# A two-layer hybrid decoder trunk on one core: layer A's column pairs in seven block products over 12 of 16 k tiles, in two chunks, and the output projections' operands split tile by tile behind the tile ahead

## The chip, the cores and the metric

The kernel runs on one core of a Trainium2 chip. The metric is the device time of one execution in microseconds, the median of several runs. The engines are TensorE (PE; its weight loads are listed as PEld), VectorE (DVE), ScalarE (ACT), GpSimd (POOL) and SyncE (SP), which issues most DMAs.

## The reference

Residual stream of 16 meta tokens and 512 tokens, 2048 channels, 16 heads of 128, float32. Layer A projects to q, f, i and z (four times 2048 columns), runs a gated linear recurrence in chunks of 64, normalizes each head, multiplies by a gate and projects back. Then a shared projection to K, V and forget logits, and layer B, attention with a forget bias, gated and projected back.

```python
def hgrn2_mix(h, g_norm, w_in, g_out, w_out, lb):
    u = rms_norm(h, g_norm) @ w_in
    q, f, i, z = ...                       # 2048 columns each
    fg = lb + (1.0 - lb) * jax.nn.sigmoid(f)
    logf, k, v = jnp.log(fg), 1.0 - fg, i
    ...                                    # chunks of 64, state carried from chunk to chunk
    o = rms_norm(o, g_out.reshape(HG_HEADS, HG_VDIM)).reshape(bsz, L, D_MODEL)
    return (o * jax.nn.silu(z)) @ w_out
```

## The kernel before, in words

**Products.** A float32 product is made of three fp32r matmuls: each operand is split into a high part (ScalarE, a copy that rounds: `w_hi`, `sh`) and a low part (VectorE, the difference: `w_lo`, `sl`), and high x high, high x low and low x high are summed in PSUM (`mm_step`, `mms`). The weights are stationary, 128 x 128; the moving operand is the transposed stream, 16 k tiles of 128 x 528 (`movx`), taken in two halves of 264 columns (`r` 0 and 1).

**Column pairs.** `run_pair` computes two 128-column outputs at once. Over the first 2 x KS = 8 k tiles it pairs even and odd k tiles, the two halves and the two columns, and takes seven block products in place of eight (sums of weight blocks `w_sum` t1 to t4 on one side, sums of the stream `S_a` on the other); over the other 8 it multiplies plainly (`rest`). Layer A takes its columns head by head: (f, i) and (q, z) of heads 2 to 14 are pairs, so are (q, z) of head 1 and (f, q) of head 15; the other columns of heads 0, 1 and 15 are plain (`run_ntiles`).

**Weights.** `Weights` streams blocks of up to 128 x 512 float32 through eight raw buffers (`w_raw`, SyncE's queue, in a fixed order), makes the sums (`get_t1`, `get_t2`, `get_t4`: VectorE, but t2's second step on GpSimd, `s.ge`), splits each unit (`split_one`, `flush`), and hands it to TensorE (`get`). A raw buffer is loaded again when the last unit that reads it is split. Units are split ahead by `split_ahead` = 2 and the extra slots of `more` (3 in layer A).

**Order.** All engines but SyncE keep the order in which the code is written out, and that is set by a planner: after each few matmuls `tick` lets `W.step` emit weight work and then each generator in `bg` (the steps of the recurrence: `head_f`, `head_q`, `head_z`, `mix`, `head_pe1`, `head_pe2`) emit as much as `fits`. A generator that needs a tile in use waits with `take`; a product that needs one calls `spin`.

**Sums of the stream.** `sums_a` (`pair_sums`) builds them once, while heads 0 and 1 run.

**Output projections.** The gated heads `G[k]` are the moving operand of layer A's output projection (`movg`) and the stationary one of layer B's (`movo`). `LazySplit` splits them: `movg.upto(NH - 1)` takes 15 of them in one go after the last product of layer A, and `movo` takes each when `o_step` asks for it, two ahead.

Of the kernel before, what the change touches and what calls it, by code (L numbers as in the profile page):

```python
# [7 lines left out]
F32 = mybir.dt.float32  # L8
# [18 lines left out]
KS = 4  # L27
KB = 4
# [191 lines left out]
class Weights:  # L220
# [59 lines left out]
    def add_pair(self, w, c, kps, rest):  # L280

        b = {}

        def block(e, n):
            b[e, n] = self.add_src(
                w[:2 * kps * P, c[n]:c[n] + P].rearrange("(j e p) n -> e p j n", e=2, p=P)[e], kps, P)

        m = kps * P
        key = len(self.units)
        t3, t2 = (key, 3), (key, 2)  # L290

        def plain(e, n):
            return self.add_unit(lambda s: s.raw[b[e, n]], [b[e, n]], m, P)
# [5 lines left out]
        def get_t2(s):  # L299
            for t in (t3, t2):  # L300
                s.sums[t] = s.alloc(f"w_sum{t[1]}", 512, F32)
            op(s.ve, s.sums[t3], s.raw[b[1, 1]], s.raw[b[0, 1]], ALU.subtract)
            return op(s.ge, s.sums[t2], s.sums[t3], s.raw[b[0, 0]], ALU.add)

        def get_t1(s):
            return op(s.ve, s.raw[b[0, 1]], s.raw[b[0, 1]], s.raw[b[0, 0]], ALU.subtract)

        def get_t4(s):
            t = s.sums.pop(t2)
            return op(s.ve, t, s.raw[b[1, 0]], t, ALU.subtract)  # L310

        block(0, 0)
        us = [plain(0, 0)]
        block(1, 1)
        block(0, 1)
        us.append(self.add_unit(get_t2, [b[1, 1], b[0, 1], b[0, 0]], m, P))
        us.append(self.add_plain(*rest[0][0]))
        us.append(self.add_unit(lambda s: s.sums.pop(t3), [], m, P))
        us.append(self.add_unit(get_t1, [b[0, 1], b[0, 0]], m, P))
        block(1, 0)  # L320
        us.append(plain(1, 0))
        us.append(self.add_plain(*rest[0][1]))
        us.append(self.add_unit(get_t4, [b[1, 0]], m, P))
        us.append(self.add_plain(*rest[1][0]))
        us.append(plain(1, 1))
        us.append(self.add_plain(*rest[1][1]))
        return us
# [103 lines left out]
    def step(self):  # L431
# [58 lines left out]
def trunk(  # L490
# [29 lines left out]
    def plan(key, w, c0):  # L520
        nt_unit[key] = [W.add_plain(*t) for t in column(w, c0)]

    def plan_pair(key, w, c):
        nt_unit[key] = W.add_pair(w, c, KS, [column(w, c0, k0=2 * KS) for c0 in c])

# [5 lines left out]
    for h in range(1, NH):  # L531
# [3 lines left out]
        for j, n in ((1, 2), (0, 3))[h == 1:] if h < NH - 1 else ((1, 0),):  # L535
            plan_pair(("a", h, j), awi, [j * D + h * P, n * D + h * P])
    for j in (2, 3):
        plan(("a", NH - 1, j), awi, j * D + (NH - 1) * P)
# [168 lines left out]
    pjb = [0]  # L707
    par = [0]
# [62 lines left out]
    def run_ntiles(keys, mov, nhalf, after=None):  # L771
# [11 lines left out]
        for u in range(nu):  # L783
            parts = [W.get(nt_unit[key][u]) for key in keys]
            for k4 in range(kts):
                k = u * kts + k4
# [3 lines left out]
                for (hi, lo, width), pt in zip(parts, pts):  # L790
                    mm_step(pt, width, (hi, lo), k4, width, xh, xl, k == 0, k == KT - 1, nhalf)
# [5 lines left out]
    def run_pair(key, mov, S_, scale, pool, tags, widths=(L, L), after=None):  # L797
# [1312 lines left out]
```

## Time and profile before

| what | value |
|---|---|
| median of 3 runs | 2013.81 us (2009.59 to 2014.51) |
| the profiled execution | 2009.89 us, span 2008.2 us |
| TensorE busy | 1980.4 us, 99% of the span, 14604 matmuls |
| VectorE, ScalarE, GpSimd busy | 1573.1 (78%), 1000.5 (50%), 319.6 us (16%) |
| granted TensorE clock, mean | 0.997 of full speed |

Layer A's heads lie from about 40 to 838 us, its output projection and what hangs on it from there to about 1050, the K/V columns up to about 1400, layer B to 1825, and its output projection at the end. A row with an arrow reads: output written from inputs; the shape is partitions x elements. In the timeline the bracket names the idle time of the engine before the row and what ended it. All instructions are put down to one line, that of the helper which issues them, so they are told apart by their tiles.

### The profile page before, as it was taken

The page shows a single profiled execution, that of the slowest core. Times are in us where ns is not written, and L with a number is a line of the kernel's source. Part 1 is how long each engine was busy: PE and PEld are TensorE (multiplying, and loading weights), DVE is VectorE, ACT ScalarE, POOL GpSimd, SP SyncE. Part 2 cuts the span into 40 slices and gives each one's busy share as a digit, 9 for nine tenths or more (in the row PEclk, how much of TensorE's full clock was granted, in tenths as well). Part 3 has the DMA queues.
Part 4 walks back from the last instruction along what each step waited for, and adds up shares of the span by engine and source line. Part 5 has one row for each costly group of instructions (what it writes and reads, how often), then busy time and mean ns, then how long its engine had stood idle before and what let it go on. Part 6 is the DMA issues. An engine that isn't in the chain of part 4 may idle for free.

```text
span 2008.2 us, 39614 instructions
## 1 busy us (share of the span) xinstructions
PE 1980.4 (99%) x14604; PEld 1851.0 (92%) x14604; DVE 1573.1 (78%) x3153; ACT 1000.5 (50%) x1869; POOL 319.6 (16%) x429
## 2 busy tenths in 40 slices
PE   8999999999999999999999999999999999999999
PEld 7999999999999999889999999999788888887888
DVE  6878888888888887788788887868677777776965
ACT  6655454545454545544343333323666666666532
POOL 2121111111111111111210000000211111220011
PEclk9999999999999999999999999999999999999999
DMA  8343333434343433446563445446556555565552
GB/s 268 101 113 109 107 112 103 116 101 119 99 120 99 120 99 104 147 132 179 163 197 98 114 123 140 117 119 184 157 159 172 157 155 164 164 166 141 147 167 91
DMA packets 455492, 273.39 MB, mean 136 GB/s; under 512 B 78065, under 2 KB 420577, under 8 KB 455281
## 3 DMA queue, kind: packets, MB, share of 16 engines
q1 hardware_dynamic: 453728, 266.33, 46.6%
q0 software_dynamic: 1536, 4.52, 0.6%
q8 instruction: 115, 1.88, 0.4%
q14 instruction: 81, 0.66, 0.1%
q10 hardware_dynamic: 32, 0.01, 0.0%
HBM read 222.46 MB, written 48.28 MB: 135 GB/s over the span
## 4 chain that ended last, share of the span: by engine, by line
PE 80%; DVE 6%; DMA 5%; ACT 4%; issue 3%; SPq 2%; POOL 0%; ACTq 0%; DVEq 0%; POOLq 0%
PE pj L196 74%; SPq L196 2%; PE o L196 2%; DMA py<-pd 2%; PE tr L196 2%; PE pat L196 2%; DVE w_lo L196 1%; ACT w_hi L196 1%; DVE lg L196 1%; DVE sm L196 1%; DMA pd<-py 1%; DVE kl L196 1%; DMA w_raw<-in_a_w_in_dram 1%; ACT lg L196 1%; ACT D L196 1%
## 5 line engine op out<-in xcount | busy, mean ns | idle before, releaser
L196 PE MATMUL pj<-sh,w_hi 128*128 128x264 f32 (+1 forms) x2484 | 750.2, 315 | 5.2 <-ACT sh L196 2.2
L196 PE MATMUL pj<-sh,w_lo 128*128 128x264 f32 (+1 forms) x2484 | 732.5, 308 | 2.4 <-DVE w_lo L196 2.4
L196 PE MATMUL pj<-sl,w_hi 128*128 128x264 f32 (+1 forms) x2484 | 733.3, 308 | 1.5 <-DVE sl L196 1.5
L196 DVE TENSOR_TENSOR w_lo<-w_raw,w_hi 128x512 fp32r<-128x512 f32 x585 | 429.7, 743 | 84.2 <-ACT w_hi L196 82.3
L196 PEld LDWEIGHTS pj<-sh,w_hi 128*128 128x128 f32 x2484 | 456.8, 189 | 27.7 <-ACT sh L196 3.2
L196 PEld LDWEIGHTS pj<-sh,w_lo 128*128 128x128 f32 x2484 | 455.8, 189 | 24.8 <-DVE w_lo L196 3.1
L196 PEld LDWEIGHTS pj<-sl,w_hi 128*128 128x128 f32 x2484 | 456.6, 189 | 20.4 <-DVE sl L196 2.5
L196 ACT ACTIVATE w_hi<-w_raw 128x512 fp32r<-128x512 f32 x585 | 354.6, 621 | 146.2 <-PE pj L196 104.3
L196 PE MATMUL pj<-sm,w_hi 128*128 128x264 f32 x896 | 172.2, 289 | 0.0
L196 ACT ACTIVATE w_hi<-w_sum 128x512 fp32r<-128x512 f32 x120 | 74.5, 626 | 179.2 <-POOL w_sum L196 93.4
L196 PE MATMUL pj<-kh,w_lo 128*128 128x264 f32 x556 | 142.7, 285 | 0.8 <-DVE w_lo L196 0.8
L196 PE MATMUL pj<-kh,w_hi 128*128 128x264 f32 x556 | 143.5, 286 | 0.0
L196 PE MATMUL pj<-kl,w_hi 128*128 128x264 f32 x556 | 142.8, 285 | 0.0
L196 PEld LDWEIGHTS pj<-sm,w_hi 128*128 128x128 f32 x896 | 138.5, 188 | 1.4
L196 PE MATMUL pj<-sm,w_lo 128*128 128x264 f32 x448 | 127.6, 285 | 0.0
L196 POOL TENSOR_TENSOR w_sum<-w_sum,w_raw 128x512 f32<-128x512 f32 x34 | 51.8, 1522 | 456.0 <-DVE w_sum L196 252.6
L196 ACT ACT_TABLE_LOAD x88 | 112.9, 1283 | 5.9 <-issue 3.1
L196 DVE TENSOR_TENSOR w_lo<-w_sum,w_hi 128x512 fp32r<-128x512 f32 x120 | 90.3, 757 | 13.5 <-ACT w_hi L196 12.6
L196 PEld LDWEIGHTS pj<-kh,w_lo 128*128 128x128 f32 x556 | 98.4, 188 | 1.3 <-DVE w_lo L196 1.3
L196 PEld LDWEIGHTS pj<-kh,w_hi 128*128 128x128 f32 x556 | 98.4, 189 | 0.0
L196 PEld LDWEIGHTS pj<-kl,w_hi 128*128 128x128 f32 x556 | 98.3, 188 | 0.0
L196 PE MATMUL pj<-kh,sh 128*128 128x264 f32 x324 | 87.6, 286 | 0.0
(403 smaller groups left out, 3568.2 us busy)
## 6 DMA issues: line engine op xcount, KB each, us to landing
w_raw<-in_a_w_in_dram SPq DMA_DIRECT2D x256, 256.0 KB, 3.4
w_raw<-in_kv_w_dram SPq DMA_DIRECT2D x128, 256.0 KB, 4.1
w_raw<-in_b_w_in_dram SPq DMA_DIRECT2D x128, 256.0 KB, 3.3
w_raw<-in_a_w_out_dram SPq DMA_DIRECT2D x64, 256.0 KB, 3.8
w_raw<-in_b_w_out_dram SPq DMA_DIRECT2D x64, 256.0 KB, 3.9
xr<-xT SPq DMA_DIRECT2D x16, 264.0 KB, 3.7
h1T<-h SPq DMA_DIRECT2D x16, 264.0 KB, 2.1
kT<-kn SPq DMA_DIRECT2D x16, 264.0 KB, 2.4
```

Source lines behind the costliest of these rows:

```text
L196: ins = f(*args, **kw)
```

## The change

Layer A's pairs take the seven products over 2 x KA = 12 k tiles and the rest over 4. A block of six k tiles is too wide for one buffer, so it comes in two chunks of 128 x 384, and every sum and split is made per chunk; the second chunk's t2 is on VectorE alone, and block (1, 1) is loaded a second time for the last product. Extra slots go from 3 to 2, and sums may be made four units ahead instead of two (in all stages). Head 1 becomes plain in all four columns. The stream's sums are kept for six tile pairs, the fourth of them in place of the even tiles' second halves, which no pair uses (`fourth_sums`, behind head 1; head 2's first pair waits for it in `late`), and head 15's plain column i starts with k tiles 12 to 15 while these halves are made anew from `xT` (`restored`). `head_z` uses the tile `bl` under the token `mixed` in place of a tile of its own. Both output projections' operands are split by a generator (`early`) during the last product ahead: tile k once TensorE's written order has passed k + 1. Pending blocks of layer B's output are counted one by one.

```diff
+KA = 6
 def add_pair(self, w, c, kps, rest):
+        chunks = range(-(-kps // 4))
+        nk = kps // len(chunks)
+        m = nk * P
         def block(e, n):
+            for x in chunks:
+                rows = w[2 * nk * P * x:2 * nk * P * (x + 1), c[n]:c[n] + P]
+                b[e, n, x] = self.add_src(rows.rearrange("(j e p) n -> e p j n", e=2, p=P)[e], nk, P)
+        def get_t2(s, x):
+            for t in (3, 2):
+                s.sums[key, t, x] = s.alloc(f"w_sum{t}{x}", m, F32)
+            op(s.ve, s.sums[key, 3, x], s.raw[b11[x]], s.raw[b[0, 1, x]], ALU.subtract)
+            return op(s.ge if x == 0 else s.ve, s.sums[key, 2, x], s.sums[key, 3, x], s.raw[b[0, 0, x]], ALU.add)
...
+        us += units(get_t4, (1, 0))
+        us.append(self.add_plain(*rest[1].pop(0)))
+        if again:
+            block(1, 1)
+        us += plain(1, 1)
 def step(self):
-            elif self.nr < min(max(self.nh, self.ns + 1) + 2, end + 2, len(self.units)) and self.sums_fit():
+            elif self.nr < min(max(self.nh, self.ns + 1) + 4, end + 4, len(self.units)) and self.sums_fit():
...
+            plan(("a", h, 0), awi, h * P)
+            plan(("a", h, 3), awi, 3 * D + h * P)
+            continue
+        for j, n in ((1, 2), (0, 3)) if h < NH - 1 else ((1, 0),):
+            plan_pair(("a", h, j), awi, [j * D + h * P, n * D + h * P], KA)
+    plan(("a", NH - 1, 2), awi, 2 * D + (NH - 1) * P, KT // UK - 1)
 def run_pair(...):
+        rest(p2, x1, True, () if more else (1,))
+        if late:
+            late()
+        product(p2[0][:, :HALF], s(1, 1), False, not more)
+    def sums_in_place():
+        for i in range(KA):
+            ...
+            yield from parts_of(sa, st[0], st[1])
+            yield from parts_of(xe[:, r0], st[2], st[3])
+    def fourth_sums():
+        for i in range(KA):
+            yield from take("os")
+            ...
+            yield from do(act, hi, x[:, r0], AF.Copy)
+            yield from do(ve.tensor_tensor, lo, x[:, r0], hi.bitcast(F32), op=ALU.subtract)
+    def restored():
+        for i in range(KA):
+            hi, lo = (t[:, HALF:] for t in movx[2 * i])
+            yield from do(act, hi, rx[i], AF.Identity, scale=g)
+            yield from do(ve.scalar_tensor_tensor, lo, rx[i], g, hi.bitcast(F32), ALU.mult, ALU.subtract)
 def head_z(hd, uz):
-        while sums in bg:
-            yield
-        sz = tl("sz")
+        yield from take("mixed")
+        sz = tl("bl")
...
+        free_u("mixed")
 class LazySplit(list):
+        def early(self, n):
+            for k in range(n):
+                while not self.stop and (at_k[0] <= k + 1 or k not in G):
+                    yield
+                if self.stop:
+                    return
+                ...                         # high part on ScalarE, low part on VectorE
...
-            W.more(lambda n, w, dt: sp.tile([P, w], dt, name=n, tag=n), 3, nt_unit["a", NH - 1, 1][-1] + 1)
+            W.more(lambda n, w, dt: sp.tile([P, w], dt, name=n, tag=n), 2, nt_unit["a", NH - 1, 1][-1] + 1)
...
+            movg = LazySplit(L)
+            movg.begin(NH - 1)
             (pt,) = run_ntiles([("a", h, 3)], movx, 2)
-    movg = LazySplit(L)
+    movg.end()
     movg.upto(NH - 1)
...
+        if slot == len(border) - 1:
+            at_k[0] = 0
+            movo = LazySplit(S)
+            movo.begin(NH // 2)
```

What stands in a row on VectorE in the middle of layer A, at the first products of a pair (f, i), before. `w_sum` is a sum of weight blocks, the second of the two made on GpSimd and not seen here; `e`, `kp`, `dp`, `uq` are steps of the recurrence:

```order
L196 TENSOR_TENSOR w_sum_6485<-w_raw 128x512
L196 SCALAR_TENSOR_TENSOR e_6276<-skf,lbt,e_6276 128x528
L196 SCALAR_TENSOR_TENSOR kp<-skf,lbt,bl 128x528
L196 TENSOR_TENSOR dp<-eb 128x4
L196 TENSOR_TENSOR uq<-pj_6304,uq 128x264
L196 TENSOR_TENSOR uq<-pj_6305,uq 128x264
L196 TENSOR_TENSOR uq<-uq,R 128x528
L196 TENSOR_TENSOR w_lo_6522<-w_sum_6486,w_hi_6521 128x512
L196 TENSOR_TENSOR w_lo_6531<-w_raw,w_hi_6530 128x512
L196 TENSOR_TENSOR w_raw<-w_raw 128x512
L196 STREAM_TRANSPOSE y0k<-kp 128x32
L196 STREAM_TRANSPOSE yk<-kp 128x3x4x32
```

And after, at the same place:

```order
L197 TENSOR_TENSOR w_lo_6969<-w_raw,w_hi_6968 128x384
L197 SCALAR_TENSOR_TENSOR e_6697<-skf,lbt,e_6697 128x528
L197 TENSOR_TENSOR w_sum_7002<-w_raw 128x384
L197 TENSOR_TENSOR w_sum_7014<-w_raw 128x384
L197 TENSOR_TENSOR w_sum_7015<-w_sum_7014,w_raw 128x384
L197 TENSOR_TENSOR uz<-pj_6958,uz 128x264
L197 TENSOR_TENSOR uz<-pj_6959,uz 128x264
L197 TENSOR_TENSOR uz<-uz,R 128x528
L197 TENSOR_TENSOR w_lo_7041<-w_sum_7003,w_hi_7040 128x384
L197 TENSOR_TENSOR w_lo_7050<-w_sum_7015,w_hi_7049 128x384
L197 TENSOR_TENSOR w_raw<-w_raw 128x384 x2
L197 TENSOR_TENSOR w_lo_7071<-w_raw,w_hi_7070 128x512
```

Where one sum of 512 stood, there are three of 384, and every low part of a sum comes twice; the steps of the recurrence (`kp`, `dp`) have moved behind them.

On ScalarE at the end of layer A, before (the last four of 15 splits of `g` that stand together, and what follows; `sz` is the last head's gate, `w_hi` are the output projection's weights):

```order
L196 ACTIVATE sh11_11552<-g11_11133 128x528
L196 ACTIVATE sh12_11556<-g12_11135 128x528
L196 ACTIVATE sh13_11560<-g13_11137 128x528
L196 ACTIVATE sh14_11564<-g14_11273 128x528
L196 ACTIVATE w_hi0_11651<-w_raw_11274 128x512
L196 ACTIVATE w_hi1_11660<-w_raw_11331 128x512
L196 ACT_TABLE_LOAD
L196 ACTIVATE sz_11612<-uz_11505 128x528
L196 ACTIVATE w_hi2_11674<-w_raw_11382 128x512
L196 ACTIVATE w_hi3_11706<-w_raw_11425 128x512
```

After, the same splits (`sh4` to `sh12`), while the last product runs; `w_hi` are that product's units and the first of the projection, `osq` the last head's output:

```order
L197 ACTIVATE sh4_12270<-g4_11927 128x528
L197 ACTIVATE w_hi2_12287<-w_raw_11999 128x512
L197 ACTIVATE sh5_12292<-g5_11929 128x528
L197 ACTIVATE sh6_12302<-g6_11931 128x528
L197 ACTIVATE sh7_12317<-g7_11933 128x528
L197 ACTIVATE sh8_12321<-g8_11935 128x528
L197 ACTIVATE sh9_12333<-g9_11937 128x528
L197 ACTIVATE w_hi3_12345<-w_raw_12073 128x512
L197 ACTIVATE sh10_12351<-g10_11939 128x528
L197 ACTIVATE sh11_12363<-g11_11941 128x528
L197 ACTIVATE osq_12376<-os_12373 128x528
L197 ACTIVATE sh12_12379<-g12_11943 128x528
```

They stand ahead of `osq` and among the last product's weights, where all 15 stood behind `osq`.

On ScalarE at the end of layer B, before; `buz` is the last gate's sigmoid, `lg` the softmax exponentials of the last head, `sh` the splits that the output projection needs first:

```order
L196 ACTIVATE lg,sm<-lg,sm 128x144
L196 ACTIVATE aos<-o 128x512
L196 ACTIVATE lg,sm<-lg,sm 128x272
L196 ACT_TABLE_LOAD
L196 ACTIVATE buz<-pj_24330 128x512
L196 ACTIVATE sh_24545<-g_19910 128x512
L196 ACTIVATE sh_24549<-g_20190 128x512
L196 ACTIVATE sh_24553<-g_20417 128x512
L196 ACTIVATE w_hi_24562<-w_raw 128x512
L196 ACT_TABLE_LOAD
L196 ACTIVATE lg,sm<-lg,sm 128x400
```

After:

```order
L197 ACTIVATE w_hi_25313<-w_raw 128x512
L197 ACTIVATE sh_25321<-g_21975 128x512
L197 ACTIVATE aos<-o 128x512
L197 ACTIVATE sh_25343<-g_22327 128x512
L197 ACTIVATE sh_25350<-g_22675 128x512
L197 ACTIVATE sh_25354<-g_22973 128x512
L197 ACT_TABLE_LOAD
L197 ACTIVATE buz<-pj_25165 128x512
L197 ACT_TABLE_LOAD
L197 ACTIVATE lg,sm<-lg,sm 128x144
L197 ACTIVATE w_hi_25392<-w_raw 128x512
L197 ACTIVATE lg,sm<-lg,sm 128x272
```

The splits and the sigmoid stand ahead of the exponentials, which stood in front of both.

## Rows read from the trace of the kernel before

**Rows 1.** Windows: stretch, length; busy us (count) PE, PEld, DVE, ACT, POOL; clock, DMA.

```profile
251.64:756.22 504.58, 504.58 (x4303) 488.54 (x4302) 413.49 (x801) 253.03 (x431) 99.16 (x100) 1.00 0.38 109
1120.00:1160.00 40.00, 40.00 (x332) 40.00 (x331) 34.58 (x76) 14.96 (x31) 2.67 (x4) 1.00 0.41 115
865.00:895.00 30.00, 30.00 (x251) 30.00 (x251) 29.03 (x50) 13.13 (x23) 5.03 (x3) 1.00 0.46 139
```

**Rows 2.** Timeline of DVE: start us, us, instruction; two scans, ten heads apart.

```profile
251.64 1.26 DVE L196 TENSOR_TENSOR_SCAN b<-cmask,sf 128x528 f32<-128x528 f32 x1 [1.45 <-ACT sf L196]
...
756.22 1.26 DVE L196 TENSOR_TENSOR_SCAN b<-cmask,sf 128x528 f32<-128x528 f32 x1 [1.45 <-ACT sf L196]
```

**Rows 3.** Groups of DVE, 200 to 800 us: xcount | busy us, mean ns | idle.

```profile
L196 DVE TENSOR_TENSOR w_lo<-w_raw,w_hi 128x512 fp32r<-128x512 f32 x190 | 136.9, 731 | 23.0 <-ACT w_hi L196 23.0
L196 DVE TENSOR_TENSOR w_lo<-w_sum,w_hi 128x512 fp32r<-128x512 f32 x71 | 54.2, 763 | 11.6 <-ACT w_hi L196 11.0
L196 DVE TENSOR_TENSOR w_sum<-w_raw,w_sum 128x512 f32<-128x512 f32 x24 | 21.3, 889 | 0.0
L196 DVE TENSOR_TENSOR w_sum<-w_raw 128x512 f32<-128x512 f32 x23 | 15.8, 688 | 0.5 <-DMA w_raw<-in_a_w_in_dram 0.5
```

**Rows 4.** Timeline of DVE, two neighbours of 512 columns, and 384 before 528.

```profile
322.11 0.53 DVE L196 STREAM_TRANSPOSE yk<-kp 128x384 f32<-128x384 f32 x1
322.57 0.66 DVE L196 TENSOR_TENSOR uq<-uq,sf 128x528 f32<-128x528 f32 x1
...
340.33 0.68 DVE L196 TENSOR_TENSOR w_sum<-w_raw 128x512 f32<-128x512 f32 x1
340.94 0.68 DVE L196 TENSOR_TENSOR w_lo<-w_raw,w_hi 128x512 fp32r<-128x512 f32 x1
```

**Rows 5.** Waits of DVE, 200 to 800 us: us in total, times, longest.

```profile
DVE w_lo L196 <- ACT w_hi L196: 34.0, 33, 2.9
DVE st L196 <- PE tr L196: 28.0, 12, 4.8
DVE b L196 <- ACT sf L196: 19.6, 11, 2.2
```

**Rows 6.** Groups of POOL and of ACT, 200 to 800 us, as rows 3.

```profile
L196 POOL TENSOR_TENSOR w_sum<-w_sum,w_raw 128x512 f32<-128x512 f32 x23 | 34.3, 1490 | 352.3 <-DVE w_sum L196 205.7 <-ACT bl L196 146.6
...
L196 ACT ACT_TABLE_LOAD x34 | 43.6, 1283 | 0.6
```

**Rows 7.** Timeline of PE where layer A's output projection begins, the waits.

```profile
839.33 0.51 PE L196 MATMUL pj<-sh,w_hi 128*128 128x264 f32 x2 [0.54 <-ACT sh L196]
840.91 0.52 PE L196 MATMUL pj<-sl,w_hi 128*128 128x264 f32 x2 [1.07 <-DVE sl L196]
...
847.33 0.51 PE L196 MATMUL pj<-sh,w_hi 128*128 128x264 f32 x2 [0.58 <-ACT w_hi L196]
850.17 0.51 PE L196 MATMUL pj<-sh,w_lo 128*128 128x264 f32 x2 [2.08 <-DVE w_lo L196]
...
861.32 0.51 PE L196 MATMUL pj<-sh,w_hi 128*128 128x264 f32 x2 [1.63 <-ACT sh L196]
```

**Rows 8.** Windows, behind these waits (columns of rows 1).

```profile
850.00:855.00 5.00, 4.83 (x27) 4.83 (x28) 3.04 (x5) 2.08 (x3) 2.49 (x1) 0.66 0.72 205
```

**Rows 9.** Timelines of ACT and DVE at that place: the splits, the norm.

```profile
838.66 8.11 ACT L196 ACTIVATE sh<-g 128x528 fp32r<-128x528 f32 x15
...
840.17 9.35 DVE L196 TENSOR_TENSOR sl<-g,sh 128x528 fp32r<-128x528 f32 x15
...
851.24 0.72 DVE L196 TENSOR_REDUCE part<-oss 128x17 f32<-128x544 f32 x1
```

**Rows 10.** Layer B's output projection: PE's two waits, the window behind them.

```profile
1828.54 0.51 PE L196 MATMUL pj<-w_hi,sh 128*128 128x512 f32 x1 [2.44 <-ACT sh L196]
...
1829.83 0.50 PE L196 MATMUL pj<-w_hi,sl 128*128 128x512 f32 x1 [0.56 <-DVE sl L196]
...
1830.00:1835.00 5.00, 5.00 (x16) 3.94 (x17) 4.12 (x10) 3.70 (x8) 0.00 (x0) 0.66 0.48 126
```

More of the change, by code (lines that the diff above doesn't have):

```diff
@@ L312, in add_pair, with get_t1, get_t4 @@
+        def get_t1(s, x):
+            return op(s.ve, s.raw[b[0, 1, x]], s.raw[b[0, 1, x]], s.raw[b[0, 0, x]], ALU.subtract)
+        def get_t4(s, x):
+            t = s.sums.pop((key, 2, x))
+            return op(s.ve, t, s.raw[b[1, 0, x]], t, ALU.subtract)
+        again = len(chunks) > 1
+        rest = [list(r) for r in rest]
         block(0, 0)
-        us = [plain(0, 0)]
+        us = plain(0, 0)
         block(1, 1)
+        b11 = [b[1, 1, x] for x in chunks]
         block(0, 1)
-        us.append(self.add_unit(get_t2, [b[1, 1], b[0, 1], b[0, 0]], m, P))
@@ L813, in product @@
         def product(o, xs, first=True, last=True):
-            w = W.get(next(us))
             for i, xx in enumerate(xs):
-                mms(o, w, i, xx, first and i == 0, last and i == KS - 1)
+                if i % nk == 0:
+                    w = W.get(next(us))
+                mms(o, w, i % nk, xx, first and i == 0, last and i == kps - 1)
                 if i % 2:
@@ L834, in done @@
             return u
-        x1, x2 = 2 * KS, 2 * KS + UK
+        x1, x2 = 2 * kps, 2 * kps + UK
+        more = x2 < KT
         pa_, p1 = pj2(), pj2()
@@ L855, in run_pair @@
         add(half(u2, 1), pb[1][:, :HALF], half(u1, 1))
-        product(p1[0][:, :HALF], x(1, 0), False, False)
-        rest(p1, x2, False, (0,))
+        product(p1[0][:, :HALF], x(1, 0), False, not more)
+        if more:
+            rest(p1, x2, False, (0,))
         product(p1[1][:, :HALF], x(1, 1), False)
@@ L989, in __getitem__ @@
             return list.__getitem__(self, k)
+    class Restored(list):
+        def __getitem__(self, k):
+            while k % 2 == 0 and k // 2 < KA and k // 2 >= back_n[0]:
+                spin()
+            return list.__getitem__(self, k)
+    back_n = [0]
     movx = LazyX()
@@ L1354, in trunk @@
             bg.append(tok_major(next(first), 4, "v", hd, "vtok"))
-            while sums in bg:
-                spin()
-            second = run_pair(("a", h, 0), movx, S_a, R, pa, ("uq", "uz"))
+            if h == 1:
+                second = plain(h, (0, "uq"), (3, "uz"))
+            else:
+                second = run_pair(("a", h, 0), movx, S_a, R, pa, ("uq", "uz"), kps=KA)
             bg.append(mix(hd, next(second)))
             bg.append(head_z(hd, next(second)))
+            if h == 1:
+                while sums in bg:
+                    spin()
+                bg.append(fourth)
         else:
@@ L1363, in trunk @@
             gp.append(opened(st_r, "gates_a", side="right"))
+            rx = [gp[0].tile([P, HALF], F32, name=f"rx{i}", tag=f"rx{i}") for i in range(KA)]
+            for i in range(KA):
+                sy.dma_start(rx[i], xT[2 * i][:, HALF:])
+            back = restored()
+            bg.append(back)
             for k, d in gd.items():
@@ L1956, in finish @@
     def finish(n, pts):
-        adding.append(n)
+        adding.extend((n, b) for b in range(4))
         yield from residual(n)
@@ L2008, in wide @@
                 spin()
-            while n == NB3 and NB3 - 1 in adding:
+            while (NB3 - 1, len(pp)) in adding:
                 spin()
```

186 lines of the change are left out of this document (109 added, 77 removed).

## The prediction

> **What bounds the kernel now.** I read the windows first, then the groups of one stage, then the waits. In the ten heads of layer A from 251.64 to 756.22 us TensorE is busy for the whole stretch, and so it is in a stretch of the next stage that holds only 264-column matmuls: 332 in 40 us, 0.1205 us each [rows 1]. The kernel is bound by the number of matmuls. The same row has the second number that counts here: VectorE is busy 413.49 us of those 504.58. The scans that open and close the stretch are ten heads apart [rows 2], so a head takes 50.46 us, of which VectorE works 41.35 and idles 9.11. TensorE stands still in two places only: where the output projection of layer A begins, and where that of layer B begins [rows 7, 8, 10].
>
> **Fewer matmuls.** A pair with seven products over 8 k tiles costs 7 x 4 x 3 = 84 matmuls and 8 x 2 x 2 x 3 = 96 for the rest, 180; over 12 k tiles it costs 7 x 6 x 3 = 126 and 48, 174. 27 pairs (two in each of heads 2 to 14, one in head 15) lose 6 each. Head 1's second pair becomes two plain columns, 192 instead of 180. That is -162 + 12 = -150 matmuls, and the order of the two programs differs by the same 150 rows on TensorE. At 0.1205 us: **-18.1 us**, if TensorE stays fed. A head of two pairs would then take 50.46 - 12 x 0.1205 = 49.0 us.
>
> **What that costs VectorE.** The mean of a group is not what an instruction costs in a queue: a 512-column one took 0.68 us, but the next started 0.61 us after it [rows 4]. So I take 0.08 off each mean of [rows 3]: 0.65 for a low part from a raw block, 0.68 from a sum, 0.81 for the last sum (its mean is lifted by GpSimd, below) and 0.61 for the other two. A 384-column instruction started its successor after 0.46 instead of 0.60, so a piece of three k tiles is 0.13 us cheaper than one of four, not a quarter cheaper [rows 4]. Before, a pair has 8 x 0.65 + 3 x 0.68 + 0.81 + 2 x 0.61 = 9.3 us. After, it has two low parts of 512 and eight of 384 from raw blocks (1.3 + 4.2), six of 384 from sums (3.3), and seven sums of 384, since the second chunk's second sum moves from GpSimd to VectorE (2 x 0.68 + 5 x 0.48 = 3.8): 12.5 us. That is +3.2 us in a pair, 6.4 in a head: VectorE needs 41.35 + 6.4 = 47.7 us of the 49.0. GpSimd gives back a little: its 512-column sum of 1.49 us [rows 6] becomes one of 384, an eighth of its work in a head at most, and the stretch it causes in VectorE's instructions shrinks with it; I count 0.3 us and end at **47.4 of 49.0, 97%**.
>
> So the gain hangs on whether VectorE can live with 1.6 us of idle time in a head where it now has 9.11. Most of that idle time is harmless: in 600 us 34.0 were low parts waiting for ScalarE's high part, which waits until TensorE frees a slot; VectorE is ahead there, and such waits shrink when it is not [rows 5]. The wait of the scan for ScalarE is another kind: VectorE scales uf, ScalarE runs two sigmoids, a table load and a logarithm, and VectorE waits 19.6 us in 11 heads, 1.8 each, with two or three other instructions in between. In the order after, some heads have 4 to 17 instructions there, and some still only two, of 384 columns: these will wait about as long. The nearest row for a loaded VectorE is 865 to 895 us: 29.03 of 30 us busy, also 97%, and TensorE busy throughout [rows 1]. It lasted 30 us, not 600. The look-ahead shrinks as well: the weights may be 5 units beyond the current one before and 4 after (two extra slots instead of three), and most units shrink from 12 matmuls to 9, so 4 x 9 x 0.12 = 4.3 us stand where 5 x 12 x 0.12 = 7.2 stood. Between nothing (the row at 97%) and +2.4 us in a head (were the waits of scan and state, 1.8 and 2.3 us, kept in full: 47.4 + 4.1 - 49.0 = 2.5) I take 0.5, nearer to the row that shows this load: 13 x 0.5 = **+6.5 us**, ends 0 and +32.
>
> One mechanism speaks against a fuller VectorE. The last sum of a pair, which stands beside GpSimd's, takes 0.889 us, its like elsewhere 0.688 [rows 3]. GpSimd works 9.9 us in a head [rows 1], and VectorE is busy 82% of the time; if it never rests, some 1.8 us more of GpSimd's work meet it, and if each costs it half its length (an estimate), its load is 47.4 + 0.9 = 48.3 us. The Trainium skill, "GPSIMD Engine Reference", section "Key points", says the same in general: GpSimd shares its SBUF interfaces with VectorE and contends with instructions that have two SBUF inputs; by that rule the trace's 0.2 us is contention, and the rival below that fills VectorE has it as one of its causes.
>
> **ScalarE, queues, start.** ScalarE gets 14 high parts of 384 and two of 512 instead of 11 of 512, and 20 more table loads; it worked 253 us of 504 [rows 1], and 2.4 us of parts and 20 x 1.28 us of loads in 13 heads [rows 6] make some 4.4 us more in a head: covered. SyncE issues four more weight loads in each pair, and the block (1,1) is read twice, 19% more bytes, at a DMA share of 0.38: covered, as long as the eight raw buffers come free in time (a rival). The sums of x grow from four to six tile pairs and the fourth sums come in head 2: by the start distances above some 12 us more VectorE work in heads 0 to 2, where head 1, now all plain, spares 4.4 and the 9 us of idle time in a head cover the rest; but head 2's first pair waits for the fourth sums before its last product: 0 to +5, I take +1. In head 15 six halves are restored (ScalarE and VectorE, 264 columns, under 0.4 us each) while the product starts at k tile 12, 24 matmuls ahead: 0 to +3, I take +1.
>
> **Layer A's output projection.** Now 15 high parts (8.11 us) and 15 low parts (9.35 us) run in one lump after the last product [rows 9]; the weights' parts stand behind the lump, and TensorE waits 0.54 + 1.07 + 0.58 + 2.08 = 4.3 us [rows 7], then runs at 1.2 GHz for part of 850 to 855: a mean clock of 0.66 means 3.4 us at half speed, 1.7 us lost [rows 8]. The last head's norm waits behind the lump too (its partial sums start at 851.24, [rows 9]), which ends in TensorE's wait of 1.63 at 861.32 [rows 7]. In the order after, twelve of the 15 stand ahead of the last head's output copy, among the last product's weights. All of 4.3 + 1.7 + 1.9 would be -7.9; VectorE has 9.4 us to place within some 12 us of the last product, so I take **-7**, ends 0 and -8.
>
> **Layer B's.** TensorE waits 2.44 + 0.56, then has the half clock for 3.4 us, 1.7 lost [rows 10]: 4.7 us. After, eight tiles are split ahead of the last gate's sigmoid, and that sigmoid ahead of the softmax exponentials; 8 tiles are 20 us of matmuls. **-4.5**, ends 0 and -5. The finer bookkeeping of pending output blocks, and the sums taken up to four units ahead in the other stages, I cost at nothing: TensorE does not wait there.
>
> **The sum**, against the profiled execution of 2009.9: -18.1 + 6.5 + 1 + 1 - 7 - 4.5 = -21.1, so 1988.8. The median of the three runs, 2013.8, lies 3.9 above the profiled one; I add about 1 and forecast **1990 us**.
>
> **Rivals.** *TensorE stays fed*: 97% is enough, as from 865 to 895. Then 6.5 + 2 us do not arise, and the time is 2009.9 - 18.1 - 12 = 1980. *VectorE becomes the bound, mildly*: the waits of scan and state stay, 4.1 us in a head; the head takes 51.5, 13 x 2.5 = 32 us take the place of 6.5: 2014, no change. Against it: those waits shrink when VectorE is late. *VectorE becomes the bound, in earnest*: the overlap with GpSimd brings its load to 48.3 and half of the present idle time, 4.5 us, stays, because an in-order queue also waits for ScalarE, which has the 20 table loads more in front of its high parts. A head takes 52.8, 13 x 3.8 = 49 us replace 6.5: 2031, slower. The point from which it decides: 13 x (head - 49.0) > 18.1 + 11.5 - 2 + 6, a head of over 51.6 us. *The chunks do not stream*: six of eight raw buffers are held by three blocks of two chunks, so loads come late and the products wait for data; one wait of 1 us in each of 26 pairs gives 2010. *The early splits do not help*: they push the last weights' parts back, the stops remain: 2000.
>
> **How the numbers follow.** Forecast 0.46 (1983 to 2000), TensorE fed 0.20, mild bound or late chunks 0.18, bound in earnest 0.10, no help from the early splits 0.06. A measurement of this kernel can tell about 0.3%, 6 us, from no change: faster means below 2007.8. The first two and the last are faster, and some of the mild cases: faster 0.76, within 0.3% 0.13, slower 0.11. The range leaves out half of the fed case's lower side and the case in earnest: 1977 to 2017.
>
> **What would show it.** Ten heads in layer A, from scan to scan, in 490 to 496 us with VectorE busy over 465; waits of TensorE for low parts in that stretch of some 5 us in all. No lump of 15 splits, no stop over 1 us and no half clock where the two output projections begin. I am wrong if the ten heads take over 505 us, if VectorE is busy for under 450 us there, or if a stop of TensorE on a weight load appears.

## The result: slower, and the profile after

| what | before | after |
|---|---|---|
| median | 2013.2 us (2009.6 to 2014.5, 4 runs) | 2041.3 us (2040.0 to 2042.4, 4 runs) |
| ratio, 95% interval | 1 | 1.0145 (1.0129 to 1.0161) |
| profiled execution, span | 2008.2 us | 2040.7 us |
| matmuls | 14604 | 14454 |

The changed kernel is 28 us slower; the forecast was 1990, the range ended at 2017. The 150 matmuls are gone, and the time is lost elsewhere. To see where, I cut both traces at the same piece of work: the matmuls of 264 columns are counted in order, so the first of each head is known (the first stands at 11.2 us in before, and the last of head 15 ends at about 839), then the first logits' matmul and the last one of layer B.

| stretch | before | after | difference | forecast |
|---|---|---|---|---|
| heads 0 to 14 of layer A | 768.2 | 790.1 | +21.9 | -9.9 |
| head 15 | 60.0 | 71.9 | +11.9 | +0.3 |
| layer A's output projection and K/V | 588.4 | 580.7 | -7.7 | -7 |
| layer B's columns and attention | 398.0 | 404.3 | +6.3 | 0 |
| layer B's output projection | 178.2 | 178.9 | +0.7 | -4.5 |

The windows over ten heads, from a scan to the one ten heads later, answer to [rows 1, 2] (stretch, length; busy us and count of PE, PEld, DVE, ACT, POOL; clock, DMA share, GB/s). The second and third row are short stretches in there.

```profile
263.37:780.10 516.73, 502.72 (x4193) 482.14 (x4193) 468.22 (x985) 304.01 (x549) 90.51 (x99) 0.99 0.42 122
315.00:325.00 10.00, 7.78 (x36) 7.07 (x35) 9.15 (x21) 6.34 (x11) 0.08 (x1) 0.66 0.36 106
547.00:555.00 8.00, 6.43 (x37) 6.13 (x38) 7.80 (x19) 5.39 (x12) 1.61 (x2) 0.79 0.66 180
```

A head takes 51.7 us, where 49.0 were to be had and 50.46 were needed before. VectorE's load is the one forecast, 46.8 us a head, and it keeps 4.85 us of idle time. TensorE, never idle there before, stands still for 14.0 us, and behind some of the stops it runs at half clock (0.66 over ten microseconds means 6.8 us at 1.2 GHz). In heads 2 to 14 such stretches add up to 27.3 us, 13.7 us lost. What TensorE waits for, from 200 to 800 us (us in total, times, longest), and what VectorE waits for there, as in [rows 5]:

```profile
PE pj L197 <- DVE w_lo L197: 9.1, 12, 1.7
PE pj L197 <- ACT w_hi L197: 7.0, 4, 2.2
PE tr L197 <- DVE bm L197: 0.6, 1, 0.6
```

```profile
DVE w_lo L197 <- ACT w_hi L197: 18.5, 22, 4.5
DVE b L197 <- ACT sf L197: 8.9, 6, 2.4
DVE st L197 <- PE tr L197: 6.0, 4, 3.9
DVE w_sum L197 <- DMA w_raw<-in_a_w_in_dram: 5.4, 5, 2.5
```

All but 0.6 us of TensorE's waits are for parts of weights. Read by itself, this looks like my rival "VectorE becomes the bound, in earnest": load as forecast, half of the idle time kept, a head over 51.6. The experiments show that it is not.

**One stop in the timelines.** SyncE, VectorE, ScalarE and TensorE about 545 us: the first pair of head 10, whose first product starts at 544.06 (start us, us, instruction; in brackets the idle time before it):

```profile
538.80 0.40 SPq L197 DMA_DIRECT2D w_raw<-in_a_w_in_dram  x1
...
540.71 0.96 SPq L197 DMA_DIRECT2D w_raw<-in_a_w_in_dram  x2
```

```profile
543.52 0.52 DVE L197 TENSOR_TENSOR w_sum<-w_raw 128x384 f32<-128x384 f32 x1
543.96 0.70 DVE L197 TENSOR_TENSOR uq<-uq,sf 128x528 f32<-128x528 f32 x1
544.58 0.77 DVE L197 TENSOR_TENSOR uz<-pj,uz 128x264 f32<-128x264 f32 x2
545.38 0.72 DVE L197 TENSOR_TENSOR uz<-uz,R 128x528 f32<-128x528 f32 x1
546.12 1.00 DVE L197 TENSOR_TENSOR w_lo<-w_sum,w_hi 128x384 fp32r<-128x384 f32 x1
547.05 1.09 DVE L197 TENSOR_TENSOR w_sum<-w_raw 128x384 f32<-128x384 f32 x1
548.17 0.86 DVE L197 TENSOR_TENSOR w_sum<-w_sum,w_raw 128x384 f32<-128x384 f32 x1
...
549.68 0.56 DVE L197 TENSOR_TENSOR w_lo<-w_sum,w_hi 128x384 fp32r<-128x384 f32 x1
```

```profile
549.12 0.52 ACT L197 ACTIVATE w_hi<-w_sum 128x384 fp32r<-128x384 f32 x1 [2.07 <-DVE w_sum L197]
```

```profile
547.18 0.39 PE L197 MATMUL pj<-sah,w_lo 128*128 128x264 f32 x1 [0.31 <-DVE w_lo L197]
...
549.70 0.59 PE L197 MATMUL pj<-sah,w_hi 128*128 128x264 f32 x1 [1.39 <-ACT w_hi L197]
```

The two chunks of block (0,1) are issued at 538.80 and 540.71 (the first of two loads there) and need some 2.8 us to land, the page's median for these loads. The sums t3 and t2 of the second chunk, at 547.05 and 548.17, stand in VectorE's queue behind a step of the recurrence (`uq`) and the evacuation of the pair before (`uz`); t2 ends at 549.03, its high part begins at 549.12, and TensorE, which had no other work from about 548.3 on, resumes at 549.70.

VectorE did not stand waiting for this block: the second piece had landed at 543.28, 3.8 us before its t3 began. So it is in most late units (defined below): in the 20 of after the piece had landed 0.02 to 7.4 us, 2.4 in the median, before its t3. A sum is written out only after its load, so a load that is issued late puts the sum late into VectorE's order, and what stands ahead of it there takes the rest of the time. GpSimd adds to it: in 14 of the 20 some instruction between t3 and the low part took 0.4 to 1.3 us longer in all beside one of GpSimd (last section). No run took GpSimd's work away, and none put the sums ahead of the evacuation with eight buffers.

Two figures measure this in every kernel, for the 24 pairs of heads 3 to 14. The *lead* is the time from the issue of the last piece of block (0,1) to the first matmul of the t2 unit made of it. The *reserve* is the time from the end of a low part to the first matmul that reads it; a unit is late when it is under 0.3 us.

| kernel | lead, median (least) | late t2 units | other late units | heads 0 to 14 | head 15 | ratio to before |
|---|---|---|---|---|---|---|
| before | 23.2 (20.8) | 0 of 24 | 0 of 240 | 768.2 | 60.0 | 1 |
| after | 10.3 (6.1) | 20 of 48 | 4 of 336 | 790.1 | 71.9 | 1.0145 |
| 1 one chunk | 19.8 (11.8) | 0 of 24 | 0 of 240 | 770.8 | 70.3 | 1.0035 |
| 2 light VectorE | 11.9 (6.8) | 25 of 48 | 0 of 336 | 780.6 | 69.2 | 1.0096 |
| 3 not restored | 10.0 (5.8) | 20 of 48 | 6 of 336 | 784.1 | 65.0 | 1.0112 |
| 4 before, loaded | 24.7 (12.4) | 0 of 24 | 0 of 240 | 790.2 | 61.8 | 1.0138 |
| 5 five slots | 8.9 (4.5) | 16 of 48 | 8 of 336 | 786.3 | 67.4 | 1.0098 |
| 6 no table loads | 9.3 (6.1) | 21 of 48 | 4 of 336 | 788.4 | 62.9 | 1.0103 |
| 9 twelve raw | 20.1 (16.2) | 5 of 48 | 3 of 336 | 771.6 | 68.2 | 1.0039 |
| 10 eleven raw | 15.4 (13.6) | 10 of 48 | 13 of 336 | 769.8 | 70.1 | 1.0028 |
| 11 and borders | 14.6 (11.4) | 15 of 48 | 21 of 336 | 772.7 | 61.7 | 1.0011 |
| 12 thirteen raw, no slot | 18.3 (15.4) | 17 of 48 | 59 of 336 | 802.8 | 62.4 | 1.0198 |

Fed throughout, the changed program's heads 0 to 14 would take 768.2 - 18.8 + 1.4 = 750.8 us: 26 pairs of heads 2 to 14 with 6 matmuls less, head 1 with 12 more, at 0.1205.

The stretches are of one execution each. Run 3 has after's instructions in the same order up to head 15, and its heads 0 to 14 still take 6.0 us less: where TensorE stops, executions of one program differ by that much, and smaller differences in this column tell nothing. Kernels without stops agree closely (768.2, and 768.7 and 768.3 in runs 7 and 8).

### The profile page after: what moved, and what is told of

Same layout as the page of the kernel before. It is cut to its first block, busy times and chain, and to the rows that moved or that the text cites. A ratio compares the mean times of both kernels' runs of the same rounds, so it can differ in the third digit from the quotient of the medians.

```text
span 2040.7 us, 40182 instructions
## 1 busy us (share of the span) xinstructions
PE 1987.1 (97%) x14454; PEld 1847.9 (91%) x14454; DVE 1655.0 (81%) x3424; ACT 1070.0 (52%) x2036; POOL 311.3 (15%) x428
## 4 chain that ended last, share of the span: by engine, by line
PE 50%; DVE 7%; ACT 4%; DMA 4%; issue 2%; SPq 1%; ACTq 0%; POOL 0%; DVEq 0%; POOLq 0%
PE pj L197 47%; DVE w_lo L197 2%; DMA py<-pd 1%; SPq L197 1%; PE o L197 1%; PE s L197 1%; DVE sm L197 1%; ACT w_hi L197 1%; DVE lg L197 1%; ACT L197 1%; ACT D L197 1%; DVE w_sum L197 1%; PE tr L197 1%; DMA g<-gd 0%; PE pat L197 0%
## 5 line engine op out<-in xcount | busy, mean ns | idle before, releaser
L197 PE MATMUL pj<-sl,w_hi 128*128 128x264 f32 (+1 forms) x2396 | 706.5, 310 | 3.4 <-DVE sl L197 3.4
L197 PE MATMUL pj<-sh,w_lo 128*128 128x264 f32 (+1 forms) x2396 | 706.2, 310 | 1.1 <-DVE w_lo L197 0.7
L197 DVE TENSOR_TENSOR w_lo<-w_raw,w_hi 128x512 fp32r<-128x512 f32 (+1 forms) x639 | 430.3, 685 | 74.7 <-ACT w_hi L197 68.7
L197 ACT ACTIVATE w_hi<-w_raw 128x512 fp32r<-128x512 f32 (+1 forms) x639 | 366.3, 586 | 200.3 <-PE pj L197 134.5
L197 ACT ACTIVATE w_hi<-w_sum 128x384 fp32r<-128x384 f32 (+1 forms) x198 | 102.7, 537 | 95.2 <-DVE w_sum L197 44.7
L197 DVE TENSOR_TENSOR w_lo<-w_sum,w_hi 128x384 fp32r<-128x384 f32 (+1 forms) x198 | 117.2, 614 | 8.4 <-ACT w_hi L197 8.0
L197 PE MATMUL pj<-sah,w_lo 128*128 128x264 f32 x324 | 96.4, 298 | 11.2 <-DVE w_lo L197 10.8
L197 PE MATMUL pj<-sah,w_hi 128*128 128x264 f32 x324 | 97.8, 302 | 7.3 <-ACT w_hi L197 7.2
L197 PE MATMUL pj<-sal,w_hi 128*128 128x264 f32 x324 | 94.1, 290 | 0.0
L197 POOL TENSOR_TENSOR w_sum<-w_sum,w_raw 128x384 f32<-128x384 f32 (+1 forms) x33 | 42.1, 1276 | 305.9 <-DVE w_sum L197 148.8
```

The source lines that it names most:

```text
L197: ins = f(*args, **kw)
```

## The experiments

My theory after the first look was VectorE's load; its rivals were the stream of weights (slots, or raw buffers) and ScalarE's table loads. `before` ran beside every group of runs; its medians lay between 2008.7 and 2010.3.

**1. The enlargement undone.** A second edit, not shown here, takes the tile `g` of a gated head only once its product fits.

```diff
-KA = 6
+KA = 4
...
```

> The changed kernel with its pairs back at seven products over 8 of 16 k tiles, in one chunk (324 matmuls more in heads 2 to 15 than with 12, since 27 pairs get 6 more each, 162 in number of products' matmuls, so 19.5 us of TensorE). Everything else of the change stays: plain head 1, fourth sums in place, restored halves, early splits. If the wider pairs are the cause of the loss in heads 2 to 14 (by VectorE's load or by the shorter stream of weights, both theories agree here), these 13 heads fall from 672 to about 656 us, and the whole from 2041 to 2021..2025, with the extra of head 15 left. If something else of the change is the cause (the fourth sums, the gate's tile), the 13 heads stay near 672 + 18 = 690 and the whole goes to some 2058.

Measured: ratio 1.0035 (1.0022 to 1.0048). Heads 0 to 14 take 770.8 us, TensorE has no wait from 180 to 800, and VectorE works 419.93 of 500 us. So the enlargement alone costs 790.1 - 770.8 = 19.3 us where it was to give 18.8, and the other edits in these heads (plain head 1, fourth sums of four tile pairs, the gate's tile) cost 770.8 - 768.2 = 2.6, of which 1.4 are matmuls. Head 15 stays long.

**2. VectorE relieved, stream as it is.**

```diff
 def get_t1(s, x):
+    if again:
+        return s.raw[b[0, 1, x]]
...
     t = s.sums.pop((key, 2, x))
+    if again:
+        return t
```

> The changed kernel with two of the four weight sums of layer A's pairs left out (t1 and t4, in both chunks: 8 VectorE instructions of 384 columns in a head, 3.8 us of VectorE); the units then hold wrong weights, with the same loads, splits, chunks and slots. VectorE-load theory: the load falls from 46.8 to 43 us in a head, about that of before, TensorE's stops in heads 2 to 14 mostly go, these 13 heads take 638..650 us instead of 672, the whole 2007..2019. Stream theory (units of 9 matmuls, two extra slots, six of eight raw buffers held): the stream is as it was, the heads stay at 668..672, the whole at 2036..2041.

Measured: ratio 1.0096 (1.0081 to 1.0111), between the two. The heads are not alike: heads 4 to 7 take 48.9 to 49.9 us, head 8 56.0, heads 9 to 14 all 51.9 or 52.0. The windows:

```profile
200.00:380.00 180.00, 179.06 (x1515) 173.62 (x1514) 158.23 (x336) 104.06 (x198) 29.19 (x34) 1.00 0.44 127
620.00:680.00 60.00, 58.10 (x487) 55.64 (x486) 50.50 (x112) 34.18 (x66) 7.75 (x10) 1.00 0.39 114
```

VectorE is busy 88% where TensorE is fed and 84% where a head takes 52.0: load is not what decides. All late units are t2 units, 25 of 48. The load theory falls, without a clear rival yet.

**3. No restored halves.**

```diff
-            for i in range(KA):
-                sy.dma_start(rx[i], xT[2 * i][:, HALF:])
-            back = restored()
-            bg.append(back)
+            back_n[0] = KA
```

> The changed kernel with the restored halves left out: head 15's columns i and z are multiplied with the fourth sums in place of x there, so they are wrong. No re-loads of x and no six pairs of splits in head 15. If the wait for the restored halves is what makes head 15 12 us longer than before, head 15 falls from 72 to 60..63 us and the whole from 2041 to 2029..2032. If head 15 is late because its pair starves like the others and because the gated heads' loads push the weights back, it stays at 68..72 and the whole at 2037..2041.

Measured: ratio 1.0112 (1.0095 to 1.0129). Head 15 takes 65.0 us instead of 71.9, between the two expectations: the restored halves cost 6.9. The rest of its excess lies in its pair (a stop of 1.9 us for a low part, one of 0.9 for a high part, 3.4 us of half clock), as in the pairs before it.

**4. VectorE loaded in the kernel before.**

```diff
-            self.ve.tensor_tensor(lo, t, hi, op=ALU.subtract)
+            for _ in range(1 + (self.ns in self.twice)):
+                self.ve.tensor_tensor(lo, t, hi, op=ALU.subtract)
...
+            W.twice.update(nt_unit[key][i] for i in (1, 3, 5, 7, 9))
```

> The kernel before with five low parts of each of layer A's pairs computed twice (the same subtraction a second time, ten more VectorE instructions of 512 columns in a head of two pairs, 6.1 us): VectorE's load goes from 41.4 to 47.5 us in a head, that of the changed kernel, but blocks, chunks, slots, buffers and matmuls stay as before. VectorE-load theory: TensorE stops at the weights' parts, the 13 heads rise from 656 to 675..690 us, the whole from 2013 to 2033..2047. Stream theory: the heads stay at 656..661, the whole at 2013..2018.

Measured: ratio 1.0138 (1.0123 to 1.0153), the whole as the load theory had it, heads 2 to 14 at 671.4 just below its range, and by another way. The window over ten heads, and TensorE's waits from 180 to 800:

```profile
260.00:780.00 520.00, 511.24 (x4308) 493.30 (x4307) 488.35 (x906) 269.48 (x449) 103.24 (x100) 0.99 0.37 106
```

```profile
PE tr L196 <- DVE bm L196: 8.7, 5, 3.3
PE pat L196 <- POOL qc L196: 0.5, 2, 0.2
```

With VectorE busy 94% (some 48.5 us a head, 1 us more than was planned), no matmul waits for a weight; the least reserve of any unit is 3.6 us. What waits is the recurrence (transposes of `bm`), five times, with 6.8 us of half clock behind each of two of them; these two heads take 56.8 and 56.6 us, the others from head 2 on 50.2 to 51.6. So the same total came from a different stop. A full VectorE does cost time, but not at the place where the changed kernel lost it.

**5. More slots.**

```diff
-            W.more(..., 2, nt_unit["a", NH - 1, 1][-1] + 1)
+            W.more(..., 5, nt_unit["a", NH - 1, 1][-1] + 1)
```

> The changed kernel with five extra weight slots in layer A instead of two, so that the parts may stand seven units ahead of TensorE instead of four. The room is had by computing only four of the six sets of sums of the stream and using two of them twice (left out: a third of the sums that heads 0 and 1 make; products of k tiles 8 to 11 use wrong sums). VectorE's load in a head stays 46.8 us. Look-ahead theory (bursts of VectorE at the borders of the pairs, which 4 x 9 matmuls do not cover): TensorE is fed, a head falls to 49.0..49.6 us, heads 0 to 14 from 790 to 750..758, the whole from about 2037 to 1997..2005. Load theory (an in-order VectorE that works 46.8 us cannot pass a head in under 51.5, whatever the look-ahead): heads 0 to 14 stay at 780..790, the whole at 2027..2037.

Measured: ratio 1.0098 (1.0083 to 1.0113); heads 0 to 14 at 786.3. The median reserve of the other units rises from 4.1 to 5.5 us, but 16 of 48 t2 units stay late: a slot does not bring the load of a block forward, nor the sum that is written behind it. The heads are within what executions of one program differ by, so look-ahead in slots is not it.

**6. No table loads.**

```diff
-        yield from do(act, sf, uf, AF.Sigmoid)
+        yield from do(act, sf, uf, AF.Exp, scale=0.01)
...
-        yield from do(act, sz, uz, AF.Sigmoid)
+        yield from do(act, sz, uz, AF.Exp, scale=0.01)
```

> The changed kernel with the four sigmoids of each of layer A's heads replaced by exponentials of a small multiple of the same operand, which need no table load (the gates are wrong): 108 table loads become 34, none of them in heads 2 to 14. ScalarE theory (the loads in front of the weights' high parts make the low parts late): heads 0 to 14 fall from 790 to 772 or less, the whole by 18 or more. VectorE theories (load, or look-ahead): the heads stay within 6 of 790, the whole within 8 of about 2037.

Measured: ratio 1.0103 (1.0082 to 1.0123); heads 0 to 14 at 788.4, 21 of 48 late. No cost of the loads shows there. In head 15, 9.0 us go: its restored halves stood behind such a load (rows further down).

**7 and 8. The early splits, each alone in the kernel before** (`at_k` and `early` added, `movg.begin` in 7, `movo.begin` in 8).

> The kernel before with only the early splits of layer A's output projection added. As the changed kernel showed: the stretch from the output projection to the forget logits falls from 191 to 183..184 us, everything else stays; the whole is 7 us (5.5 to 8.5) below before. Rival: the early splits push the last product's weights back, head 15 grows by what is won, the whole stays within 2 of before.

> The kernel before with only the early splits of layer B's output projection and the count of pending blocks one by one. By the prediction: the stops of 2.4 and 0.6 us and the half clock behind them go, the whole falls by 4.5 us (4 to 5). By what the changed kernel's trace shows (178.9 us from the last logits' matmul to the end instead of 178.2; new stops of 3.3 us for an output tile and 1.4 us for a gate): the stops change their place and the whole stays within 1.5 of before.

Measured: 7 has ratio 0.9955 (0.9941 to 0.997), 2001.9 against 2010.3; 8 has 1.0012 (1.0002 to 1.0021), a little slower than before. Layer A's lump and its waits [rows 7 to 9] are gone; what is left from 820 to 900 us, and the window there:

```profile
PE pj L196 <- DVE h L196: 1.8, 1, 1.8
PE pj L196 <- DVE w_lo L196: 0.4, 1, 0.4
```

```profile
820.00:870.00 50.00, 50.00 (x425) 48.67 (x424) 41.42 (x80) 26.87 (x46) 3.63 (x4) 1.00 0.40 118
```

Layer B's stops [rows 10] only change their name, in 8 from 1795 to 2006 us:

```profile
PE pj L196 <- DVE ot L196: 1.9, 2, 1.4
PE pj L196 <- DVE buz L196: 1.4, 1, 1.4
PE pj L196 <- DVE w_lo L196: 0.8, 1, 0.8
```

Kernel 7 is faster than both, by 0.45% against before.

**9 and 10. More raw buffers.** `load` takes its buffer from a list of slots, to which layer A adds some (9: four of 512 columns; 10: three of 384, in place of one extra weight slot, with all results computed).

```diff
-            old = self.nd - self.raw_bufs
+            slot = next(s for s in self.cycle if s < self.raw_bufs or self.fits_extra())
+            old = self.hold.get(slot, -1)
...
+            W.more_raw(4, nt_unit["a", NH - 1, 1][-1] + 1, 512)
```

> The changed kernel with twelve raw buffers in layer A's pairs instead of eight. The room is had by computing only four of the six sets of sums of the stream and using two of them twice (left out: a third of the sums that heads 0 and 1 make; products of k tiles 8 to 11 use wrong sums). Two extra weight slots, VectorE's load and table loads as in the changed kernel. Ring theory (in the slow heads SyncE issues the second half of block (0,1) only 4 to 6 us ahead of its use, since its buffer is still read; the units made of it then have no reserve, while every other unit has 2.6 us or more): that block comes early, the stops at product s(0,1) go, heads 0 to 14 fall from 790 to 752..762, the whole to 2000..2012. Load theory (VectorE in order at 46.8 us a head): heads 0 to 14 stay at 780..790, the whole at 2028..2038.

> The changed kernel, complete in its results, with three more raw buffers of 384 columns in place of one of the two extra weight slots (eleven and one instead of eight and two). Ring theory: the block (0,1) comes early, most stops go; the slot given up costs some of the reserve of 2.6 us, but less than the ring gives: heads 0 to 14 at 755..770, the whole at 2003..2018. Look-ahead theory: one slot less makes it worse, heads 0 to 14 over 795, the whole over 2042. Load theory: 780..792, the whole 2028..2040.

Measured: 9 has ratio 1.0039 (1.0027 to 1.0051), 10 has 1.0028 (1.0017 to 1.004). The lead rises from 10.3 us to 20.1 and 15.4, and heads 0 to 14 fall from 790.1 to 771.6 and 769.8, three times what executions of one program differ by. The window of 9 and TensorE's waits from 200 to 800, against those of after above:

```profile
260.00:760.00 500.00, 495.19 (x4199) 476.70 (x4198) 473.51 (x982) 299.23 (x549) 93.30 (x100) 1.00 0.44 126
```

```profile
PE tr L197 <- DVE bm L197: 3.6, 5, 1.9
PE pj L197 <- DVE w_lo L197: 2.3, 5, 1.3
PE pj L197 <- ACT w_hi L197: 0.7, 1, 0.7
```

VectorE is busy 95%, more than in after, and heads 3 to 14 take 49.6 us on the average. TensorE's waits fall from 16.7 to 6.6 us. This settles it: the late loads of block (0,1), not VectorE's load, made most of the stops. Run 10 ends where the ring theory expected it; run 9's heads are 10 us above, its whole 6; both have a long head 2, 58.1 and 54.6 us, where TensorE waits for the fourth sums and then has the half clock (for 13.7 and 6.8 us).

**11 and 12. The two borders, and the slots again.** 11 is 10 with the fourth sums begun in head 1's last column and the restored halves first among the generators; 12 is 11 with thirteen raw buffers and no extra slot.

```diff
-            bg.append(back)
+            bg.insert(0, back)
...
         for i in range(KA):
+            while at_k[0] <= 2 * i + 1:
+                yield
```

> The changed kernel, complete in its results, with eleven raw buffers and one extra slot, and its two borders mended: the fourth sums begin behind each tile's last use in head 1's last column instead of behind the whole head, and the work on the restored halves stands first among the planner's generators instead of last. If the waits for these two (5.7 + 1.2 us of TensorE's stops in head 2 and 5.3 in head 15, each with a stretch of half clock behind it) are only a matter of their place in the queues, heads 0 to 14 fall from 770 to 760..764, head 15 from 70 to 61..65, the whole to 2000..2007, 0.2 to 0.5% below before. Rival: VectorE has no time for the fourth sums wherever they stand (24 instructions more in a stretch that is 95% busy), the stops move on into the next product: heads 0 to 14 stay at 766..770, head 15 at 66..70, the whole at 2009..2014.

> As the run before it, but with thirteen raw buffers and no extra weight slot (parts may stand two units ahead, 18 matmuls, 2.2 us). If the ring alone bounds and the slots do not matter, heads 0 to 14 are within 4 us of the run before it. If the parts' look-ahead is the next bound, TensorE stops for low parts at every border of a pair: heads 0 to 14 over 775, the whole over 2016.

Measured: 11 has ratio 1.0011 (1.0003 to 1.002), 12 has 1.0198 (1.0181 to 1.0216). In head 15 the edit does what was expected, 70.1 to 61.7 us. Head 2 falls by 2.8 us, but heads 3 to 14 take 4.5 us more. So heads 0 to 14, at 772.7, lie above both expectations, and the whole is where the rival had it, no faster than before. That the fourth sums pushed the stops into the next products, as the rival says, is not shown: 4.5 us is less than executions of one program differ by. In 12 the low parts are late all over, here from 120 to 770 us:

```profile
PE pj L197 <- DVE w_lo L197: 25.1, 44, 1.5
PE pj L197 <- ACT w_hi L197: 4.1, 5, 1.4
```

Its lead is the second longest of the kernels with twelve tiles, yet 59 of the 336 other units are late. Slots and raw buffers are two separate bounds; the change had tightened both (one slot less, and twelve loads in a pair instead of eight, through the same eight buffers), and the raw buffers were the nearer one.

## Why the prediction was wrong, step by step

**Fewer matmuls: right.** 150 are gone, and in run 9 seven of the heads 3 to 14 take 48.8 to 49.4 us, where 49.0 was worked out.

**VectorE's load: right; its +0.5 us a head agrees with run 9.** Forecast 47.4 us a head, measured 46.8 in after and 47.0 in run 9 (473.51 of 500, at 49.6 a head). There, with the blocks in time, a head takes 0.6 us more than 49.0; the term was 0.5. The 30 us stretch at 97% [rows 1] was a good row to take, but the term belongs to an order: in run 4, with 48.5 us of VectorE in before's order, a head loses 1.2.

**SyncE, "covered, as long as the eight raw buffers come free in time": the step that failed.** In the sum this step cost nothing; in the 24 pairs of heads 3 to 14 the first 54 matmuls, and what runs among them, take 28.5 us less in run 9 than in after, where these heads as a whole take 26 more. The five stretches together exceed their forecasts by 54 us, and this is more than half of it; 12 us of the rest lie in head 15 and 12 in layer B. I counted buffers, not the time that they leave: the lead falls from 23.2 to 10.3 us, and to 6.1 at the worst, against some 2.8 for the load and the chain of t3, t2, high and low part behind a burst of evacuations. I had the mechanism as a rival ("the chunks do not stream") at one wait of 1 us in each pair, 2010. That price was near on the average (28.5 / 24 = 1.2 us a pair), though the loss is uneven: against run 9, four pairs lose 4.3 to 8.8 us at this place, and no other over 2.7. What was wrong is that the forecast rested on "covered". The written order tells behind which low part each load stands; I did not work the lead out from it.

**The fourth sums, +1, and the restored halves, +1: both too small.** With four tile pairs (run 1) heads 0 to 2 take about 1 us more than the count of matmuls gives; with six, 5.7 in after, 9.4 in run 10 and 13.2 in run 9. TensorE stops in head 2 (in after 1.82 us until 153.43 and 0.87 until 154.69, with the half clock from 153.8). The restored halves cost 6.9 (run 3): their high parts stood in ScalarE's queue behind head 15's exponentials, a table load and a gate, and run 11, which puts them first, has 8.4 us of run 10's head 15 back. The rows of ScalarE and TensorE's two waits:

```profile
836.48 0.63 ACT L197 ACTIVATE bl<-bl 128x528 f32<-128x528 f32 x1
837.13 1.28 ACT L197 ACT_TABLE_LOAD   x1
838.43 0.64 ACT L197 ACTIVATE sf<-uq 128x528 f32<-128x528 f32 x1
838.98 0.63 ACT L197 ACTIVATE osq<-os 128x528 f32<-128x528 f32 x1
839.51 0.61 ACT L197 ACTIVATE w_hi<-w_raw 128x512 fp32r<-128x512 f32 x1
840.03 0.91 ACT L197 ACTIVATE sh<-rx,VA 128x264 fp32r<-128x264 f32 x2
```

```profile
840.58 0.59 PE L197 MATMUL pj<-sh,w_hi 128*128 128x264 f32 x1 [2.85 <-ACT sh L197]
843.68 0.59 PE L197 MATMUL pj<-sl,w_hi 128*128 128x264 f32 x1 [2.29 <-DVE sl L197]
```

I had counted the 24 matmuls ahead as cover and the two instructions at under 0.4 us, and left out the queue in front of them.

**Layer A's output projection, -7: right** (-7.9 from its first matmul to the forget logits; run 7 gives 8.4 in the whole).

**Layer B's, -4.5: wrong.** The stops were not the splits' alone: with these out of the way, TensorE waits for the last gate's product (`buz`) and for output tiles (`ot`). I followed the wait that ended last and did not ask what is late next. Run 8 gains nothing.

**Layer B's columns, 0: +6.3, and open.** The attention's matmuls, and SyncE's transfers up to the last columns, are written in the same order in both kernels. The stretch takes 396.4 to 399.2 us in the five kernels with eight k tiles and 399.9 to 407.5 in the nine with twelve (run 11: 401.4, run 12: 407.5). The attention's matmuls wait 3.4 us for `PTh` in after, 1.7 in before and 1.1 in run 9, which covers 1.7 of the 6.3 at most. What carries over from layer A I did not find.

**The chances.** "VectorE in earnest", at 2031, lay nearest to the result, and even its signs came (a head of 51.7 us, half of the idle time kept), but it is not what happened: that its number was near is luck. The mechanism that did happen had been put in one case with a milder one, at 2010.

## What to carry to other kernels

Where a block is cut in pieces, work out for a ring of buffers how long before its use each piece can be issued, from the instruction that frees its buffer, and compare it with load, chain and queue together; a count of buffers says little. A wait for "VectorE's low part" names the last link: before blaming the engine's load, look at whether only one kind of unit is late, and vary the load, the slots and the ring one by one. When a stop is mended, name what is late next.

## What the runs showed of the chip

An instruction of VectorE that began while one of GpSimd ran mostly waited for its end. I took the 384-column sums and low parts of heads 2 to 15 in after. The 192 low parts from raw blocks that met no GpSimd instruction took 0.55 us each (0.56 at most). Of all these sums and low parts, 84 met one. In 43 of them VectorE's took longer, up to 1.69 us; each of these had begun after GpSimd's and ended 0.41 to 0.43 us behind its end. The other 41 lost nothing: in 30 VectorE's had begun first or at the same time, and for the other 11 the trace shows no reason. The rows at 546.12 and 547.05 us above are two of the 43, beside these:

```profile
545.49 1.22 POOL L197 TENSOR_TENSOR qc<-uq,eb 128x256 f32<-128x256 f32 x1
546.66 1.05 POOL L197 TENSOR_TENSOR qp<-uq,eb 128x256 f32<-128x256 f32 x1
```

In all, VectorE lost 25.8 us in the 53.7 that the 84 spent beside GpSimd, 0.48 of it; my estimate of half the length was right on the average. The Trainium skill, "GPSIMD Engine Reference", section "Key points", names this contention for VectorE instructions with two SBUF inputs, without a size; the trace agrees in the 43.

A short stop of TensorE could cost two and a half times its length. In after it waits 2.22 us for a high part, until 317.37; from 317.6 on the clock is at 1.2 instead of 2.4 GHz for 6.8 us (the window at 0.66), 3.4 us lost on top. Many stops of under 1 us had no such stretch behind them: run 2 has 26 waits for parts from 180 to 800 us, the longest 1.4 us, and one stretch of half clock.
